# Hybrid decoder step on one core: order of splits, stores and bank copies in the first two feed-forward units

## The chip, the cores and the metric

The kernel runs on one core of a Trainium2 chip. The metric is the device time of one execution in microseconds (us); lower is better. The engines of the core run side by side, each with a queue of its own: TensorE (PE in the profile, its weight loads PEld), VectorE (DVE), ScalarE (ACT), GpSimd (POOL) and SyncE (SP). Nearly all transfers between the core's memory (SBUF) and the chip's main memory are issued from SP. PE writes its sums into eight banks of PSUM, which DVE and ACT read.

## The reference

One layer is computed for 2048 prompt rows and 64 sample rows of width 1024. After the attention half, each row x goes through a feed-forward half:

```
h = rms_norm(x, g_ffn_pre)
u = relu(h @ w_up)            # 1024 -> 4096
f = (u * u) @ w_down          # 4096 -> 1024
x = x + rms_norm(f, g_ffn_post)
```

All of it is float32. The change concerns the transition from the attention half to this one.

## The kernel before, in words

**Products in three parts.** A float32 matrix is split for PE into a high part (an ACT copy that rounds to the format of fast matmuls) and a low part (a DVE subtraction: original minus high part). A product is high*high + high*low + low*high, so each operand costs one ACT and one DVE instruction before PE can use it (split_by, L1610).

**Seven products for eight.** Both products of the feed-forward half use a seven-product scheme for 2x2 block matrices. The prompt rows are cut into two halves (sb = 0, 1) of 1024 rows; each half has 4 pairs of row tiles (row i and row i+4, 128 rows each). From the normed rows seven blocks H[1] to H[7] of 512 columns are made: four are the transposed rows themselves, three are differences; part p-1 of the row buffer ht holds block p. The weights w_up are taken 256 columns at a time (fc = 0 to 15). One (sb, fc) is a **unit**: seven products p = 1 to 7 of 12 matmuls each (up_product), p 0 and 8 being the sample rows' products and p 9 two transposes of these. Their banks appear in the profile as X (uX; products 1 and 2), Z (uc; 5 and 3), V (ud or ue by turns; 7 and 4) and Y (ua in unit 0, else ub; 6). Products 1 and 2 share a bank, as do 5 and 3, and 7 and 4; the sum after the first of them is read (by taken, L1751) before the second is added on top. So "copy X" is ACT's st<-uX, "copy Z" ACT's st<-uc. A unit's seven outputs lie in a buffer st (14 KB a partition): DVE adds up the sums (add), ACT takes relu and square (squared), and the buffer is stored to main memory (s_d) by end (L1838), which is run while the next unit's products go on.

**Weights of a unit.** Besides the two halves of the weights (which = 0 and 1; split_up, L1614) two pairs of sums are needed: sums_13, then, in the same tile, sums_24; each is split too (split_sums; tile names t and s in the profile). While unit fc runs, the function ahead (L1777) makes the weights of unit fc+1: "a" is the first half, "s13" and "s24" the sums, "13" and "24" their splits.

**Order of the queues.** te, ac and dv stand for PE, ACT and DVE with an order written out by hand: each instruction issued through them keeps its place behind the one issued before. Each engine works its queue strictly in order, so a waiting instruction holds up all that stand behind it. SP's transfers are put in order by the compiler, except where issue_after names one to follow. Waits between engines are put in by the compiler: for the data of a tile, and for a tile that takes the place of another in memory, for all users of the old one.

**The transition.** The rows come in the order 8, 12, 9, 13, 10, 14, 11, 15 for the second half, through residual (L1509): norm, 8 transposes on PE into two banks (xnT), two ACT copies from these to ht (L1536 to L1544), and for the second row of a pair four DVE differences (L1549 to L1551), then a store of ht to main memory (h_d, L1557). For each pair a new ht is taken, in the same place of pool keep as the one before (L1530), so that its first copies wait for the store. The last two rows overlap with unit 0 (sb 0, fc 0), whose order is UP_FIRST = 1, 0, 2, 8, 5, 7, 9, 6, 3, 4 and whose side work is written out in opening (L1847):
- row 11's two copies are put off (late_copies, L1542) and run at product 2, behind the first up weights' split
- row 15 (last_rows) is taken a step at a time: scaling at products 1 and 0, transposes and copies at 5, two differences at 7, the others and the store at 9
- blocks 7, 6, 3 and 4 of the first half's rows, stored earlier, are fetched and split in that order. Block 4 is fetched (L1882) into the place where its own low part will lie, H[4][1], and split in place (L1589). H[4]'s two tiles lie one behind the other in pool h_4, which takes, with h_3, the place of the row pools x (16 KB) and s (statistics of the rows) once these are closed (L1873 to L1875), and room behind them
- at product 4 the weight sums "s24", their split, and the split of the second up weights of unit 1 follow.

Unit 1 is the one case where st lies in keep, where ht was (L1741). Units 1 to 15 use UP_ORDER = 1, 5, 7, 0, 6, 8, 3, 2, 9, 4; unit 1's product 1 is issued by unit 0, behind its product 6.

Of the kernel before, what the change touches and what calls it, by code (L numbers as in the profile page):

```python
# [13 lines left out]
F32R = mybir.dt.float32r  # L14
# [127 lines left out]
def hybrid_step_kernel(ctx: ExitStack, tc: tile.TileContext, I, O):  # L142
# [1320 lines left out]

    def h_place(sb, p):

        H[p] = [h_pools[p].tile([P, KT // 2, BT], F32R, tag=f"h{p}{u}", name=f"H{p}{u}_{sb}", bufs=1) for u in range(2)]

    def open_pools(to, names, label, side="left"):
        to.update({name: open_pool(f"{label}_{name}", side) for name in names})
# [14 lines left out]
    def ht_place(name):  # L1484
        return keep.tile([P, 7, KT // 2, P], F32, tag="st", name=name, bufs=1)
# [23 lines left out]
    def residual(i, banks, tensor=nc.tensor, scalar=nc.scalar, vector=nc.vector):  # L1509

        n = rows(i)
        x = res_x.pop(i, None) or load_x(i)[0]
        ssq = sp.tile([P, 48], F32, tag="ssq", name=f"bssq_{i}", bufs=2)
        junk = sp.tile([P, D], mybir.dt.bfloat16, tag="junk", name=f"bjunk_{i}", bufs=1)
        x1 = R["x"].tile([P, D], F32, tag="x1", name=f"x1_{i}", bufs=2)
        if i == NB:
            banks = [folded(x1[:NS, c * 512 : (c + 1) * 512], p_) for c, p_ in enumerate(banks)]
        if banks:
            g = g_mix if tensor is nc.tensor else [gpost[:, c * 512 : (c + 1) * 512] for c in range(2)]
            yield from mixed(i, banks, x, x1, junk, ssq, g, sp, scalar, vector)  # L1520
        rs = ssq[:, 3:5]
        scalar.activation(junk[:n], x[:n], AF.Square, accum_out=ssq[:n, 2:3])
        yield
        rsqrt_mean(sp, rs[:n, 1:2], ssq[:n, 2:3], n, D, vector=vector)
        vector.scalar_tensor_tensor(x1[:n], x[:n], rs[:n, 1:2], gpre[:n], op0=ALU.mult, op1=ALU.mult)
        yield
        sb, j, second = i // 8, i % 4, i % 8 >= 4
        q = slice(j * P, (j + 1) * P)
        if i < NB and not second and i:
            sums[sb, j] = ht_place(f"ht_{i}")  # L1530
        for h in range(2):
            kk = slice(h * 4, h * 4 + 4)
            pt = (bank([P, 512], "ce"[h], f"xnT_{i}_{h}") if te is tensor else next_bank("cdce", f"xnT_{i}_{h}")).rearrange("p (k t) -> p k t", k=4)
            for k in range(4):
                tensor.transpose(pt[:, k, :n], x1[:n, (h * 4 + k) * P : (h * 4 + k + 1) * P], ident[:n, :n])
            if i == NB:  # L1536
                split_copy(xsT[:, kk, :NS], xsT[:, kk, NS:], pt[:, :, :NS], vector)
                continue
            ht = sums[sb, j]
            copy = (ht[:, (6, 2)[h] if second else h], pt, AF.Copy)  # L1540
            if i == B_ORDER[-2]:
                late_copies.append(copy)  # L1542
            else:
                scalar.activation(*copy)  # L1544
            if sb == 0 and not second:
                split_copy(H[h + 1][0][:, :, q], H[h + 1][1][:, :, q], pt, vector)
        if i == NB or not second:
            return
        yield  # L1549
        for out, a, b in ((4, 6, 0), (6, 2, 6), (5, 2, 4), (3, 1, 5)):  # L1550
            vector.tensor_tensor(ht[:, out], ht[:, a], ht[:, b], op=ALU.subtract)  # L1551
            if out == 6 and i == B_ORDER[-1]:
                yield
        kept = slice(2 * (sb == 0), 7)
        if i == B_ORDER[-3]:
            yield
        latest_store[:] = [nc.sync.dma_start(h_d[sb][:, kept, :, q], ht[:, kept])]  # L1557

    h_raws = {}

# [49 lines left out]
    def split_by(scalar, vector, hi, lo, src):  # L1610
        scalar.activation(hi, src, AF.Copy)
        vector.tensor_tensor(lo, src, f32(hi), op=ALU.subtract)

    def split_up(sb, fc, which, scalar=nc.scalar, vector=nc.vector):  # L1614

        w = P if sb and not which else FC
        halves_[sb, fc, which] = parts = [
            U["ab"[which] + "hl"[u]].tile([P, KT // 2, w], F32R, tag="w", name=f"w{which}{u}_{sb}_{fc}", bufs=1) for u in range(2)  # L1620
        ]
        split_by(scalar, vector, *parts, raws[sb, fc][which][:, :, :w])

    for n, i in enumerate(B_ORDER[2:]):
        early.append((i, []))
# [101 lines left out]
    def up(sb, fc, before, steps=iter(())):  # L1727
# [20 lines left out]
        def add(out, a, b, op=ALU.add):  # L1748
            dv.tensor_tensor(s(out), a, b, op=op)
# [27 lines left out]
        def ahead(kind):  # L1777

            if last:
                return  # L1780
            if kind == "a":
                split_up(sb, fc + 1, 0, ac, dv)
            elif kind in ("13", "24"):
                split_sums(sb, fc + 1, int(kind), ac, dv)
            else:
                (sums_13 if kind == "s13" else sums_24)(sb, fc + 1, dv)
# [6 lines left out]
        for p in UP_FIRST if first else UP_ORDER:  # L1793
            if (sb, fc, p) == (0, 1, 1):
                pass
            elif 0 < p < 8:
                product(p)
            elif sb:
                continue
            elif p < 9:  # L1800
                sample_up(fc, p // 8, sam)
            if p == 3:
                add(6, s(1), Z)
            if first:
                opening(p, taken, ahead)
                if p == 3:
                    squared(s(6))
                elif p == 6:
                    next(features)
                continue  # L1810
            if p == 1:
                next(before, None)
                if fc > 1 or sb:
                    split_up(sb, fc, 1, ac, dv)
                if fc + 2 < NFC:
                    load_up(sb, fc + 2)
                deque(before, 0)
            if p == 3:
                ahead("24")
                squared(s(6))  # L1820
            else:
                taken(p)
            if p == 1:
                ahead("s13")
            elif p == 7:
                ahead("13")
            elif p == (6 if sb else 0):
                ahead("a")
            if p == 6:
                ahead("s24")  # L1830
            downs(p)
            run(steps, 2)
# [3 lines left out]
        run(features)  # L1836

        def end():  # L1838
            add(1, s(1), V)
            yield  # L1840
            squared(s(1))
            add(2, s(1), s(5), ALU.subtract)
            nc.sync.dma_start(s_d[sb][fc], place[0])

        return end()

    def opening(p, taken, ahead):  # L1847

        if p == 1:
            taken(p)  # L1850
            next(last_rows)
            loaded = placing[0]
            for n, raw in enumerate(h_raws[3]):
                with tc.issue_after(loaded.ins):
                    loaded = nc.sync.dma_start(raw, h_d[0][:, 2, 2 * n : 2 * n + 2])
            next(seventh)
        elif p == 0:
            next(last_rows)
            sums_24(0, 0, dv)
        elif p == 2:  # L1860
            taken(p)
            ahead("a")
            for copy in late_copies:
                ac.activation(*copy)
        elif p == 8:
            taken(p)
            split_sums(0, 0, 24, ac, dv)
            run(load_h(0, 6, ac, dv))
            U.pop("tmp").release()
        elif p == 5:  # L1870
            taken(p)
            next(last_rows)
            close_pools(R)  # L1873
            for q in H_LATE[3:]:
                h_pools[q] = open_pool(f"h_{q}")  # L1875
            ahead("s13")
            run(load_h(0, 3, ac, dv))
            h_place(0, 4)
            loaded = None
            for k in range(0, KT // 2, 2):  # L1880
                with tc.issue_after(loaded.ins) if loaded else nullcontext():
                    loaded = nc.sync.dma_start(f32(H[4][1][:, k : k + 2]), h_d[0][:, 3, k : k + 2])  # L1882
            with tc.issue_after(loaded.ins):
                latest_store[:] = [load_up(0, 2)]
        elif p == 7:
            taken(p)
            next(last_rows)
            split_in_place(4)
        elif p == 9:
            taken(p)  # L1890
            ahead("13")
            run(last_rows)
        elif p == 6:
            next_X.append(bank([P, BT], "a", "uX_0_1"))
            up_product(0, 1, 1, next_X[0])
            taken(p)
        elif p == 3:
            with tc.issue_after(latest_store[0].ins):
                for half in range(2):
                    load_down(0, half)  # L1900
        else:
            ahead("s24")
            ahead("24")
            split_up(0, 1, 1, ac, dv)

    def sample_up(fc, c, sam):

# [350 lines left out]
```

## Time and profile before

| what | us |
|---|---|
| median of 3 runs | 2193.89 |
| lowest and highest run | 2193.14, 2196.88 |
| the profiled execution | 2193.01 |
| its span, first to last instruction | 2191.2 |
| the first units in it, from unit 0's first product to unit 2's first | 879.52 to 930.60 |

A row of the profile names the source line, engine, operation and the tiles written and read (numbers left out: H stands for all blocks, st for all unit buffers). Many instructions have line L131, that of the helper which keeps the order by hand; they are told apart by their tiles. Times are microseconds from the first instruction. In a timeline the columns are start, length, engine, line, operation and tiles, and the count that a row merges; brackets give the idle time of the engine just before, and what ended it. In a table of windows they are the stretch, its length, the busy time of PE, PEld, DVE, ACT and POOL (with counts), the granted clock of PE, the busy share of the transfer engines and the rate in GB/s. In a list of waits they are who waited for whom, the sum in us, how often, and the longest.

### The profile page before, as it was taken

What the parts mean: (1) busy time and instruction counts of PE and PEld (TensorE: products, weight loads), DVE (VectorE), ACT (ScalarE), POOL (GpSimd) and SP (SyncE); (2) the same over time, 40 slices, a digit from 0 to 9 for tenths busy, and PEclk for the clock granted to TensorE, in tenths of its full rate; (3) what the DMA queues carried; (4) which work ended last, traced back from release to release, by engine and by line L of the source; (5) the groups of instructions that cost most, each with busy time, mean ns of one, the idle gap of its engine ahead of it and who ended that gap; (6) DMA issues with size and microseconds to landing.
All of it is one profiled execution on the core that took longest, in us unless ns stands there. A gap on an engine that the chain in (4) does not pass through costs nothing.

```text
span 2191.2 us, 34210 instructions
## 1 busy us (share of the span) xinstructions
PE 2156.9 (98%) x11784; PEld 1864.8 (85%) x11784; DVE 1530.7 (70%) x3199; ACT 1219.1 (56%) x2626; POOL 257.7 (12%) x414
## 2 busy tenths in 40 slices
PE   8999999999999999999999999999999999999998
PEld 7999989999998888788888887888888888888886
DVE  5988968777785765888888555548676666555566
ACT  5888867566664444555555544435445455444454
POOL 2566512121111100000000000000000000000000
PEclk9999999999999999999999999999999999999999
DMA  7344332224337765877777776758554433766685
GB/s 229 133 144 150 103 104 66 68 71 150 131 126 239 235 205 193 263 240 257 272 258 249 249 237 220 242 181 269 179 182 158 153 136 134 241 202 195 194 271 185
DMA packets 240314, 411.54 MB, mean 188 GB/s; under 512 B 25924, under 2 KB 142124, under 8 KB 236028
## 3 DMA queue, kind: packets, MB, share of 16 engines
q1 hardware_dynamic: 240140, 409.35, 56.6%
q8 instruction: 93, 1.52, 0.3%
q14 instruction: 81, 0.66, 0.1%
HBM read 265.82 MB, written 143.99 MB: 187 GB/s over the span
## 4 chain that ended last, share of the span: by engine, by line
PE 89%; ACT 3%; DVE 3%; DMA 2%; POOL 1%; issue 1%; SPq 0%; DVEq 0%; POOLq 0%; ACTq 0%
PE dn L131 27%; PE gproj L131 11%; PE uc L131 8%; PE uX L131 7%; PE out L1328 7%; PE proj L131 5%; PE ud L131 4%; PE ub L131 4%; PE ue L131 4%; PE sam L131 1%; PE dsam L131 1%; PE o L131 1%; PE sc L131 1%; PE out L131 1%; PE av L131 1%; PE pT L131 1%
## 5 line engine op out<-in xcount | busy, mean ns | idle before, releaser
L131 PE MATMUL dn<-o0t,o0s 128*128 128x512 f32 x896 | 349.3, 390 | 2.1 <-ACT f L2026 1.0
L131 PE MATMUL dn<-o1t,o0s 128*128 128x512 f32 x896 | 349.6, 390 | 0.7 <-DVE o1t L220 0.7
L131 PE MATMUL dn<-o0t,o1s 128*128 128x512 f32 x896 | 349.4, 390 | 0.0
L220 DVE TENSOR_TENSOR o1s<-rs,o0s 128x512 fp32r<-128x512 f32 x224 | 154.6, 691 | 230.9 <-ACT o0s L219 225.1
L219 ACT ACTIVATE o0s<-rs 128x512 fp32r<-128x512 f32 x224 | 141.1, 631 | 305.3 <-PE dn L131 285.4
L131 PE MATMUL gproj<-wg,gxh 128*128 128x384 f32 x1024 | 272.5, 342 | 0.3 <-DVE gp_s L214 0.3
L131 PEld LDWEIGHTS dn<-o0t,o0s 128*128 128x128 f32 x896 | 168.2, 188 | 39.8 <-ACT o0t L219 1.6
L131 ACT ACTIVATE st<-st 128x512 f32<-128x512 f32 x224 | 141.2, 630 | 106.7 <-DVE st L131 101.9
L131 PEld LDWEIGHTS dn<-o1t,o0s 128*128 128x128 f32 x896 | 168.2, 188 | 37.7 <-DVE o1t L220 1.9
L131 PEld LDWEIGHTS dn<-o0t,o1s 128*128 128x128 f32 x896 | 168.2, 188 | 35.3
L131 PE MATMUL uc<-H,s 128*128 128x512 f32 x768 | 187.8, 393 | 2.8 <-ACT st L131 2.8
L131 PEld LDWEIGHTS gproj<-wg,gxh 128*128 128x128 f32 x1024 | 183.8, 188 | 4.1 <-issue 3.1
L131 PE MATMUL gproj<-wg,gxl 128*128 128x384 f32 x576 | 186.0, 340 | 0.4 <-DVE gp_s L214 0.4
L131 PE MATMUL uX<-H,w 128*128 128x512 f32 x768 | 185.5, 390 | 0.0
L131 PEld LDWEIGHTS uc<-H,s 128*128 128x128 f32 x768 | 143.7, 189 | 33.6 <-ACT st L131 3.0
L131 PEld LDWEIGHTS uX<-H,w 128*128 128x128 f32 x768 | 144.4, 188 | 30.5
L220 DVE TENSOR_TENSOR o1t<-rt,o0t 128x512 fp32r<-128x512 f32 x224 | 153.1, 684 | 9.0 <-ACT o0t L219 9.0
L1328 PE MATMUL out<-wo,mt 128*128 128x512 f32 x680 | 158.6, 392 | 0.0
L209 POOL TENSOR_TENSOR frs<-rs_v,half 128x1 f32<-128x1 f32 (+1 forms) x13 | 10.1, 786 | 1208.7 <-DMA rt<-t_d 1119.0
L1328 PEld LDWEIGHTS out<-wo,mt 128*128 128x128 f32 x680 | 126.5, 188 | 26.1
L219 ACT ACTIVATE o0t<-rt 128x512 fp32r<-128x512 f32 x224 | 138.1, 618 | 12.0 <-DMA rt<-t_d 8.5
L131 DVE TENSOR_TENSOR st<-st 128x512 f32<-128x512 f32 x160 | 110.6, 691 | 28.5 <-ACT st L131 24.3
(405 smaller groups left out, 4306.9 us busy)
## 6 DMA issues: line engine op xcount, KB each, us to landing
s_d<-st SPq DMA_DIRECT2D x32, 1792.0 KB, 8.1
rs<-s_d SPq DMA_DIRECT2D x224, 256.0 KB, 2.9
raw<-in_w_up SPq DMA_DIRECT2D x64, 512.0 KB, 4.4
rt<-t_d SPq DMA_DIRECT2D x128, 256.0 KB, 3.9
rt<-in_w_down SPq DMA_DIRECT2D x96, 256.0 KB, 3.0
t<-in_w_down SPq DMA_DIRECT2D x64, 256.0 KB, 3.8
t_d<-t SPq DMA_DIRECT2D x32, 512.0 KB, 4.2
hraw<-h_d SPq DMA_DIRECT2D x20, 512.0 KB, 5.1
```

The lines of the kernel that those rows point to most:

```text
L131: ins = call(*a, **k)
L209: nc.gpsimd.tensor_tensor(out, v[:n], e, op=ALU.pow)
L219: nc.scalar.activation(hi, src, AF.Copy)
L220: vector.tensor_tensor(lo, src, f32(hi), op=ALU.subtract)
L1328: te.matmul(banks[c], x, w[:, c * 512 : (c + 1) * 512], start=k + u == 0, stop=k == KT - 1 and u == len(products) - 1,)
```

## The change

- In the second row half, the pairs share one ht (no new one per pair). Parts 0 and 1 are stored as soon as the first row of a pair is copied, parts 2 to 6 after the second row; row 11's parts 0 and 1 are stored in opening. The first half's store is as it was (parts 2 to 6).
- Row 11's late copies go from product 2 to product 1, ahead of copy X.
- H[4]'s two tiles are placed in the other order, so that the fetch fills the one that lies first.
- Row 15's first two differences go from product 7 to 5 (ahead of the sums s13 and block 3's split), the last two still stand at product 9, now behind "s24", which comes up from product 4.
- The sums with Y and Z (taken(6), s(6)) and their squares go from products 6 and 3 to product 4, behind the split of the "24" weights. Of the second up weights' split, the ACT part stands ahead of them and the DVE part (split_low) behind; then comes the sum with V, which was in end.
- In unit 1, end's squares, difference and store of unit 0 go from product 1 (ahead of copy X) to product 5 (behind copy Z).

```diff
 h_place(sb, p):
-        H[p] = [h_pools[p].tile([P, KT // 2, BT], F32R, tag=f"h{p}{u}", name=f"H{p}{u}_{sb}", bufs=1) for u in range(2)]
+        H[p] = [
+            h_pools[p].tile([P, KT // 2, BT], F32R, tag=f"h{p}{u}", name=f"H{p}{u}_{sb}", bufs=1)
+            for u in ((1, 0) if (sb, p) == (0, 4) else (0, 1))
+        ]
+        if (sb, p) == (0, 4):
+            H[p].reverse()
 residual:
-            sums[sb, j] = ht_place(f"ht_{i}")
+            sums[sb, j] = sums[sb, j - 1] if sb and j else ht_place(f"ht_{i}")
         if i == NB or not second:
+            if i < NB and sb and i != B_ORDER[-2]:
+                nc.sync.dma_start(h_d[sb][:, :2, :, q], ht[:, :2])
             return
-        kept = slice(2 * (sb == 0), 7)
-        latest_store[:] = [nc.sync.dma_start(h_d[sb][:, kept, :, q], ht[:, kept])]
+        latest_store[:] = [nc.sync.dma_start(h_d[sb][:, 2:, :, q], ht[:, 2:])]
 split_up:
-        split_by(scalar, vector, *parts, raws[sb, fc][which][:, :, :w])
+        src = raws[sb, fc][which][:, :, :w]
+        if vector is None:
+            scalar.activation(parts[0], src, AF.Copy)
+        else:
+            split_by(scalar, vector, *parts, src)
+
+    def split_low(sb, fc, which, vector):
+        hi, lo = halves_[sb, fc, which]
+        vector.tensor_tensor(lo, raws[sb, fc][which], f32(hi), op=ALU.subtract)
 up:
-            if p == 3:
+            if p == 3 and not first:
                 add(6, s(1), Z)
             if first:
-                opening(p, taken, ahead)
-                if p == 3:
+                opening(p, taken, ahead, lambda out, a, b: add(out, s(a), {"Z": Z, "V": V}[b]))
+                if p == 4:
                     squared(s(6))
...
-                deque(before, 0)
+                if fc > 1 or sb:
+                    deque(before, 0)
...
+            elif p == 5:
+                deque(before, 0)
 end:
-            add(1, s(1), V)
+            if not first:
+                add(1, s(1), V)
 opening:
         if p == 1:
+            for copy in late_copies:
+                ac.activation(*copy)
+            nc.sync.dma_start(h_d[1][:, :2, :, 3 * P :], sums[1, 3][:, :2])
             taken(p)
...
         elif p == 2:
             taken(p)
             ahead("a")
-            for copy in late_copies:
-                ac.activation(*copy)
...
         elif p == 5:
             taken(p)
+            next(last_rows)
             next(last_rows)
...
         elif p == 7:
             taken(p)
-            next(last_rows)
             split_in_place(4)
         elif p == 9:
             taken(p)
             ahead("13")
+            ahead("s24")
             run(last_rows)
         elif p == 6:
             next_X.append(bank([P, BT], "a", "uX_0_1"))
             up_product(0, 1, 1, next_X[0])
-            taken(p)
...
         else:
-            ahead("s24")
             ahead("24")
-            split_up(0, 1, 1, ac, dv)
+            split_up(0, 1, 1, ac, None)
+            taken(6)
+            add(6, 1, "Z")
+            split_low(0, 1, 1, dv)
+            add(1, 1, "V")
```

More of the change, by code (lines that the diff above doesn't have):

```diff
@@ L1845, in up, with opening @@
         return end()
-    def opening(p, taken, ahead):
+    def opening(p, taken, ahead, add):
         if p == 1:
+            for copy in late_copies:
+                ac.activation(*copy)
+            nc.sync.dma_start(h_d[1][:, :2, :, 3 * P :], sums[1, 3][:, :2])
             taken(p)
```

## The prediction

> **What bounds the kernel now.** I read the page's share of busy time first, then the chain that ended last.
>
> ```profile
> span 2191.2 us, 34210 instructions
> PE 2156.9 (98%) x11784; PEld 1864.8 (85%) x11784; DVE 1530.7 (70%) x3199; ACT 1219.1 (56%) x2626; POOL 257.7 (12%) x414
> ...
> PE 89%; ACT 3%; DVE 3%; DMA 2%; POOL 1%; issue 1%; SPq 0%; DVEq 0%; POOLq 0%; ACTq 0%
> ```
>
> TensorE (PE) is busy 98% of the span, so an edit to the other engines counts only where PE stands still. The change touches the first two units (blocks 0 and 1 of the first row half, about 879 to 931 us). There I read PE's timeline; the bracket is the idle time before a group and what ended it.
>
> ```profile
> 890.93 1.14 PE L131 MATMUL xnT<-ident,x 128*128 128x128 f32 x8 [1.00 <-ACT ht L131]
> ...
> 897.64 2.92 PE L131 MATMUL uX<-H,w 128*128 128x512 f32 x12
> ...
> 912.88 0.73 PE L131 MATMUL ub<-H,s 128*128 128x512 f32 x2 [0.45 <-ACT s L131]
> 914.14 2.57 PE L131 MATMUL ub<-H,s 128*128 128x512 f32 x10 [0.53 <-DVE s L131]
> ...
> 920.42 4.34 PE L131 MATMUL uc<-H,s 128*128 128x512 f32 x12 [2.77 <-ACT st L131]
> 924.56 3.23 PE L131 MATMUL uX<-H,w 128*128 128x512 f32 x12
> ...
> 930.60 2.88 PE L131 MATMUL uX<-H,w 128*128 128x512 f32 x12
> 933.32 2.90 PE L131 MATMUL uc<-H,s 128*128 128x512 f32 x12
> ...
> 951.89 2.88 PE L131 MATMUL uX<-H,w 128*128 128x512 f32 x12
> ```
>
> Four stops: 1.00 + 0.45 + 0.53 + 2.77 = 4.75 us. They cost more than that. From 930.60 to 951.89 one whole unit without a stop takes 21.29 us, and a product of twelve matmuls 933.32 - 930.60 = 2.72. From 897.64 to 930.60 PE does one unit and two products more (p3 and p4 of unit 0): 21.29 + 2 x 2.72 = 26.7, but it takes 32.96. So 6.2 us are lost there, and 1.0 at 890.93: **7.2 us** in all, 0.33% of the time. That is the ceiling of what the change can gain, because PE waits for nothing else in reach of it. The windows show what makes 7.2 out of 4.75.
>
> ```profile
> 918.10:920.42 2.32, 0.00 (x0) 0.00 (x0) 0.99 (x2) 2.23 (x4) 0.00 (x0) 1.00 1.08 351
> 920.42:924.76 4.34, 4.33 (x13) 3.45 (x14) 3.75 (x5) 2.27 (x3) 0.00 (x0) 0.66 1.03 420
> ```
>
> After the last stop the granted clock (third number from the right) is 0.66: the product at 920.42 takes 924.56 - 920.42 = 4.14 instead of 2.72, 1.4 us more, and the next some 0.3; the other 0.7 is the refilling of the pipeline at the stops. [...]
>
> **The change, part by part.** Queues of the engines are worked through in program order, by the spacings that the rows show: a VectorE (DVE) subtraction of 128x1024 takes 1.15 us of its queue, a pair of 128x512 about 1.3; on ScalarE (ACT) 1.0 and 0.5. ACT now:
>
> ```profile
> 882.57 0.60 ACT L131 ACTIVATE st<-uX 128x512 f32<-128x512 f32 x1 [1.06 <-PE uX L131]
> ...
> 890.28 1.09 ACT L131 ACTIVATE ht<-xnT 128x512 f32<-128x512 f32 x2 [1.80 <-DMA h_d<-ht]
> ...
> 891.51 1.07 ACT L131 ACTIVATE s<-t 128x1024 fp32r<-128x1024 f32 x1
> ...
> 899.98 1.06 ACT L131 ACTIVATE H<-H 128x1024 fp32r<-128x1024 f32 x1 [2.14 <-DMA H<-h_d]
> 901.83 1.06 ACT L131 ACTIVATE H<-H 128x1024 fp32r<-128x1024 f32 x1 [0.79 <-DMA H<-h_d]
> ...
> 918.11 1.29 ACT L131 ACTIVATE st<-st 128x512 f32<-128x512 f32 x2 [3.45 <-DVE st L131]
> 919.31 0.58 ACT L131 ACTIVATE st<-uX 128x512 f32<-128x512 f32 x1
> 919.78 0.59 ACT L131 ACTIVATE st<-uc 128x512 f32<-128x512 f32 x1
> ```
>
> *Row store in two parts, bank copies first.* The two copies at 890.28 (row 11) need a new row buffer, hence the landing of row 14's whole store, which is in the chain of waits:
>
> ```profile
> 881.10 9.16 DMA h_d<-ht
> ...
> 896.51 5.30 DMA H<-h_d
> ```
>
> PE's transposes of row 15 need the banks that those copies empty: that is the stop of 1.00. After the change the copies write parts 0 and 1 of the same buffer, stored long before for row 10; they wait only for row 14's subtractions (over at 881.1) and stand ahead of the uX copy, in the 1.06 us in which ACT waits for PE anyway: about 881.5 to 882.6. Without that cover they would cost 1.0. Gain **1.0**. The added stores (one each for rows 8 to 11, a quarter of a us to half a us of SP issue) carry bytes that the whole store no longer carries; the ones for rows 8 to 10 lie beside out products in which PE never stops, so I take 0. The store for row 11 stands in front of row 15's x store on SP, with no more bytes ahead of block 3's fetch than now.
>
> *Fourth block into the other half.* SP now:
>
> ```profile
> SPq L1882 <- DVE H L131: 6.3, 1, 6.3
> ```
> ```profile
> 860.69 0.55 SPq L1557 DMA_DIRECT2D h_d<-ht  x1
> ...
> 887.85 1.95 SPq L1855 DMA_DIRECT2D st<-h_d  x2
> 896.14 0.79 SPq L1882 DMA_DIRECT2D H<-h_d  x2
> ...
> 906.68 0.53 SPq L1557 DMA_DIRECT2D h_d<-ht  x1
> ```
>
> The fetch waits 6.3 us for the split of block 6, since the tile that it fills lies on that block's staging pool. By the code H[4]'s first tile begins where the pool of row statistics began, last used by row 15's scaling before 889; with the order turned, the fetch lands there. It can go right behind block 3's, about 890 (6 us earlier), and both ACT waits (2.14, 0.79) end. Transfers from SP follow each other: the engines fell idle as block 3 was in,
>
> ```profile
> 861.00:862.00 1.00, 1.00 (x6) 0.83 (x5) 0.75 (x1) 0.16 (x1) 0.00 (x0) 1.00 0.07 19
> 867.00:868.00 1.00, 1.00 (x6) 0.81 (x5) 0.23 (x2) 0.00 (x0) 0.54 (x1) 1.00 0.97 290
> ...
> 894.00:895.00 1.00, 1.00 (x7) 0.80 (x5) 1.00 (x2) 1.00 (x3) 0.00 (x0) 1.00 0.05 20
> ```
>
> so block 4 follows from 894 and is in at 897.5 (1 MB at some 350 GB/s), as ACT comes to it. By itself the edit buys no PE time; it clears the queue for the next step. If block 3's and 4's bytes mixed instead, see the third case.
>
> *Order of splits, sums and squares.* DVE now:
>
> ```profile
> 888.94 0.68 DVE L131 TENSOR_TENSOR t<-t,raw 128x512 f32<-128x512 f32 x1
> ...
> 892.62 1.23 DVE L131 TENSOR_TENSOR s<-t,s 128x1024 fp32r<-128x1024 f32 x1 [1.14 <-ACT s L131]
> 893.76 2.35 DVE L131 TENSOR_TENSOR H<-hraw,H 128x1024 fp32r<-128x1024 f32 x2
> ...
> 900.10 1.41 DVE L131 TENSOR_TENSOR ht<-ht 128x512 f32<-128x512 f32 x2
> ...
> 905.21 1.41 DVE L131 TENSOR_TENSOR ht<-ht 128x512 f32<-128x512 f32 x2
> ...
> 912.87 1.23 DVE L131 TENSOR_TENSOR s<-t,s 128x1024 fp32r<-128x1024 f32 x1 [1.19 <-ACT s L131]
> 914.01 1.22 DVE L131 TENSOR_TENSOR w<-raw,w 128x1024 fp32r<-128x1024 f32 x1
> ...
> 917.40 0.68 DVE L131 TENSOR_TENSOR st<-st,ud 128x512 f32<-128x512 f32 x1
> ```
>
> No DVE instruction is added, and on ACT none. Without the late copies in front, ACT makes the high part at 891.51 about 1.2 earlier (it needs the sums, over at 890.3), so the low part at 892.62 runs at 891.4 and block 6's at 892.6 to 894.9. PE is by then 1.0 earlier: the cover stays. Then DVE does, in the new order, row 15's first two differences (1.3), next weight sums (1.3), block 3 (2.3), V (0.6), block 4 (2.3), the 13 weights (1.15), the 24 sums (1.3) and the last differences (1.3): 11.6 us, till **906.4**. Row 15's store goes there, 0.3 before the 906.68 of now. The 24 weights' low part (ACT's high part is ready at 906) ends at 907.8; PE wants it at 912.88 - 0.45 - 1.0 = 911.4 (where it now begins to wait, less the first gain). Slack 3.6: the stops of 0.45 and 0.53 go. Then three sums of unit 0 (2.0) and the low part of the second up weights (1.15): 910.9, against PE's want at 911.4 + 2.72 = 914.1.
>
> What is late next is the stop at 920.42. PE waits there for the copy of Z (uc, 919.78), queued on ACT behind two squares (918.11), which wait 3.45 us for the V sum (917.40). In the new order ACT has the X copy and the Z copy before those squares. But the X copy opens unit 1's buffer, which lies where the row buffer lay: **a wait is added**, the landing of row 15's store, and behind it on ACT the Z copy, then the squares; PE waits for Z. The trace does not show that wait. It is bounded by two stores: 9.16 us for the one at 881.10, amid other transfers, and for the one at 860.69, alone: 1.25 us until the first byte (0.07 of slice 861 to 862), then 1.835 MB at 290 GB/s, 6.3, and some 0.5 until the waiter ran. The new store has 5 of 7 parts and finds the engines idle: 1.25 + 4.5 + 0.5 = 6.3. I take this, the nearer row: 906.4 + 6.3 = 912.7, Z copied at 913.8, and PE comes for it at 915.1 (914.1 and the samples: now from 916.7, the end of the group at 914.14, to 920.42 - 2.77 = 917.65). Slack 1.3 us. With 9.16 it is 916.7, a stop of 1.6.
>
> After that unit 1's X, Z and V sums have no new wait, and unit 0's store to memory leaves near 916 rather than 920; its buffer is next written in unit 2.
>
> **Sum:** 1.0 + 6.2 = 7.2 us. The profiled execution: span 2191.2, time 2193.01, so 2185.8; the median of the runs shown, 2193.89, is 0.88 above, and from it the forecast is **2186.7 us**.
>
> **The rivals.**
> 1. *The row buffer is late.* Store landing in 9.16, or leaving 1 to 3 us later: PE stops 1.6 to 3 us for Z, and from about 2.8 pays the slow clock (1.7) again. Gain 5.5 down to 2.5: 2188.4 to 2191.4, the shorter stops likelier, so about 2189.2. For it: slack of only 1.3. Against: the engines are empty at 906.
> 2. *DVE or ACT becomes the bound.* If block 4 and the next weights (2 MB, now issued near 890) share the engines with block 3 instead of following it, block 3 is in near 900 instead of 894; ACT and DVE stand in line behind its split, and PE's p3 of unit 0 stops 3 to 4 us, with the slow clock: 7.2 - 5.2 = 2.0, 2191.9. Against: the idle slice at 894.
> 3. *It doesn't do what it says:* the other half also touches the staging pool and the fetch goes near 895. Then block 4 is split some 1 us later, inside the slacks: still 2186.7 to 2187. It is no case of its own and counts with the forecast.
> 4. *Slower.* If the wait goes by the whole row buffer and not by its parts, the copies at the head of unit 0 hold ACT until row 14's store has landed, 890.25, and now the uX copy stands behind them: X is copied at 891.9, PE's second uX product waits from 883.3, 8.6 us, then the slow clock, 1.7. 10.3 lost against 7.2 won: +3.1, 2197.0 (a longer cold spell: up to 2199). It is slower as soon as that landing is after 887.3. Against: block 4's two halves were split each at its own transfer's end (2.14 and 0.79), so waits go by parts.
>
> **How the numbers follow.** Forecast 0.62, first rival 0.16, second 0.12, fourth 0.07, other things 0.03. The range goes from 2185.5 (all of it, and 1.2 from shorter tails) to 2191.7, in the second rival's middle: left out are the fourth, half the second and a little below, about 0.18. About 0.2% (4.4 us, below 2189.5) is what a measurement of this kernel can tell from no change. Faster: 0.62 + 0.11 of the first = 0.73. Within: 0.05 of the first, 0.12, half of the fourth = 0.20. Slower: the rest of the fourth and of the others, 0.07.
>
> **What would show it.** ACT's ht copies near 881.5 with no DMA wait, and no stop before PE's transposes; the H fetch on SP near 890; row 15's store near 906; the copy of uc near 913.5, ahead of the squares; clock 1.00 in every slice from 880 to 930; unit 2's first uX near 923.4. A PE stop at p3 of unit 1 speaks for the first rival, one at p3 of unit 0 for the second, one before the second uX for the fourth.

## The result, and the profile after

The changed kernel takes 2188.85 us (median of 9 runs, 2186.53 to 2191.24), the kernel before, run in turn with it, 2193.89 us (9 runs, 2191.23 to 2201.41). The ratio is **0.9973, 95% interval 0.9962 to 0.9985**: 3.3 to 8.3 us faster. The forecast of 2186.7 us, 7.2 below the median shown, lies inside the interval; the median came out 2.15 us above it.

The profiled execution of the changed kernel took 2191.24 us, the longest of its nine. First the page: the span, the share of the engines, and the chain that ended last.

```profile
span 2189.5 us, 34228 instructions
...
PE 2157.9 (99%) x11784; PEld 1866.5 (85%) x11784; DVE 1531.0 (70%) x3199; ACT 1218.4 (56%) x2626; POOL 257.8 (12%) x414
...
PE 89%; ACT 4%; DVE 4%; DMA 2%; issue 1%; POOL 1%; DVEq 0%; SPq 0%; POOLq 0%; ACTq 0%
```

PE's work is the same 11784 matmuls. The span is only 1.7 us shorter, so the page alone would say that most of the gain failed to come. The first two units say otherwise. This is PE's timeline of the changed kernel there:

```profile
881.52 3.02 PE L131 MATMUL uX<-H,w 128*128 128x512 f32 x12
...
891.78 1.03 PE L131 MATMUL xnT<-ident,x 128*128 128x128 f32 x8
...
898.49 2.92 PE L131 MATMUL uX<-H,w 128*128 128x512 f32 x12
...
913.12 2.91 PE L131 MATMUL ub<-H,s 128*128 128x512 f32 x12
...
917.17 3.03 PE L131 MATMUL uc<-H,s 128*128 128x512 f32 x12 [0.19 <-ACT st L131]
920.04 2.88 PE L131 MATMUL uX<-H,w 128*128 128x512 f32 x12
...
925.74 2.88 PE L131 MATMUL uX<-H,w 128*128 128x512 f32 x12
```

Of the four brackets of before (1.00, 0.45, 0.53, 2.77) one is left, of 0.19. I call the time from unit 0's first uX to unit 2's first uX **the stage**. It took 930.60 - 879.52 = 51.08 us before and takes 925.74 - 881.52 = 44.22 now, **6.86 less**; the prediction had unit 2 begin at 923.4, so 43.9. PE's clock (third number from the right in a table of windows) stays at 1.00 in it:

```profile
880.00:900.00 20.00, 20.00 (x105) 16.82 (x105) 18.39 (x25) 15.70 (x24) 1.08 (x2) 1.00 1.05 345
900.00:915.00 15.00, 15.00 (x72) 12.50 (x71) 14.61 (x19) 7.49 (x13) 0.00 (x0) 1.00 0.58 171
915.00:930.00 15.00, 14.81 (x70) 12.20 (x69) 12.17 (x18) 9.17 (x15) 0.00 (x0) 1.00 0.75 267
390.00:400.00 10.00, 10.00 (x75) 9.22 (x75) 6.32 (x18) 5.83 (x18) 1.64 (x2) 0.85 0.09 25
1520.00:1530.00 10.00, 7.94 (x28) 6.10 (x27) 8.37 (x14) 4.92 (x8) 0.00 (x0) 0.83 0.58 196
```

The last two rows are where this execution gave time back, both far from the change. At 390 to 400 PE is busy throughout, small matmuls among its work, but at a clock of 0.85; before, that stretch had 1.00. The stage starts 2.0 us later than before, so every time in it is to be read 2.0 later than in the prediction. The other loss is a stop in the second half's down products, where the same wait was 0.36 us before, with a clock of 0.83 around it:

```profile
1523.13 0.63 PE L131 MATMUL dn<-o0t,o0s 128*128 128x512 f32 x1 [2.06 <-DVE f L1976]
```

Together, 2.0 later before the stage, 6.86 won in it, and 3.2 lost behind it (the remainder) make the 1.7. Whether these losses belong to the change is the first question for the experiments.

ACT's timeline of the changed kernel answers to the one shown of before:

```profile
881.52 2.00 ACT L131 ACTIVATE H<-hraw 128x1024 fp32r<-128x1024 f32 x2
883.41 1.07 ACT L131 ACTIVATE ht<-xnT 128x512 f32<-128x512 f32 x2
884.58 0.60 ACT L131 ACTIVATE st<-uX 128x512 f32<-128x512 f32 x1
...
899.00 1.06 ACT L131 ACTIVATE H<-H 128x1024 fp32r<-128x1024 f32 x1 [0.29 <-DMA H<-h_d]
900.26 1.06 ACT L131 ACTIVATE H<-H 128x1024 fp32r<-128x1024 f32 x1 [0.20 <-DMA H<-h_d]
...
911.31 2.48 ACT L131 ACTIVATE st<-st 128x512 f32<-128x512 f32 x4 [1.91 <-DVE st L131]
...
916.03 0.60 ACT L131 ACTIVATE st<-uX 128x512 f32<-128x512 f32 x1 [1.36 <-DMA h_d<-ht]
916.53 0.59 ACT L131 ACTIVATE st<-uc 128x512 f32<-128x512 f32 x1
917.01 1.29 ACT L131 ACTIVATE st<-st 128x512 f32<-128x512 f32 x2
```

The two ht copies at 883.41 wait for nothing and fill the time in which ACT waited for PE. The copy of Z (uc) stands ahead of the squares at 917.01. In front of it is the wait that the change adds: the copy of X waits 1.36 us for the landing of the row buffer's store. SP's timeline shows that store (908.68) and the fetch of block 4 (892.09):

```profile
884.51 3.59 SPq L1870 DMA_DIRECT2D h_d<-ht  x1
...
892.09 1.24 SPq L1902 DMA_DIRECT2D H<-h_d  x2
...
906.63 0.37 SPq L1613 DMA_DIRECT2D raw<-in_w_up  x1
908.68 0.37 SPq L1563 DMA_DIRECT2D h_d<-ht  x1
```

The chain that ended last in this stretch runs through the store, once:

```profile
907.93 0.70 DVE ht L131
908.63 0.02 SPq L1563
908.65 0.03 issue
908.68 7.27 DMA h_d<-ht
...
916.03 1.09 ACT st L131 x2
917.13 0.04 issue
917.17 3.03 PE uc L131 x12
```

The store took 7.27 us, not the 6.3 forecast, and left 0.3 us later in the stage than forecast; so the slack of 1.3 us became a stop of 0.19. Two us ahead of it SP had issued another transfer, the first half of unit 3's up weights (0.5 MB, at 906.63). Before, both halves of these weights left behind the store, at 914.85; now the sums that free their place are made earlier.

### The profile page after: what moved, and what is told of

It reads as the page before. It is cut to its first block, busy times and chain, and to the rows that moved or that the text cites. A ratio compares the mean times of both kernels' runs of the same rounds, so it can differ in the third digit from the quotient of the medians.

```text
span 2189.5 us, 34228 instructions
## 1 busy us (share of the span) xinstructions
PE 2157.9 (99%) x11784; PEld 1866.5 (85%) x11784; DVE 1531.0 (70%) x3199; ACT 1218.4 (56%) x2626; POOL 257.8 (12%) x414
## 4 chain that ended last, share of the span: by engine, by line
PE 89%; ACT 4%; DVE 4%; DMA 2%; issue 1%; POOL 1%; DVEq 0%; SPq 0%; POOLq 0%; ACTq 0%
PE dn L131 27%; PE gproj L131 11%; PE uc L131 8%; PE uX L131 7%; PE out L1328 7%; PE proj L131 5%; PE ud L131 4%; PE ub L131 4%; PE ue L131 4%; PE sam L131 1%; PE dsam L131 1%; PE o L131 1%; PE sc L131 1%; PE out L131 1%; PE av L131 1%
```

## The experiments

In every expectation A is the account that the prediction gave; the other letters are the rivals, named there. The runs e1 to e4 were timed in turn with the kernel before at 2193.41 us (24 runs), e5 to e8 at 2194.14 (23 runs).

| run | median us (runs) | ratio, 95% | stage us | PE's stops in the stage |
|---|---|---|---|---|
| changed kernel | 2188.85 (9) | 0.9973 (0.9962 to 0.9985) | 44.22 | 0.19 |
| e1 changed, again | 2186.57 (7) | 0.9973 (0.9962 to 0.9983) | 44.16 | none |
| e2 row store, early copies alone | 2190.48 (10) | 0.9986 (0.9976 to 0.9995) | 48.16 | 0.25, 0.53, 2.77 |
| e3 changed, old fetch place | 2186.56 (5) | 0.9968 (0.9956 to 0.9980) | 44.24 | none |
| e4 order alone | 2189.82 (10) | 0.9984 (0.9975 to 0.9993) | 47.63 | 1.45, 1.93 |
| e5 before, stop filled | 2193.13 (10) | 0.9994 (0.9985 to 1.0003) | 49.50 | 0.91, 0.53, 0.53 |
| e6 changed, a new buffer | 2196.11 (10) | 1.0009 (1.0000 to 1.0018) | 53.02 | 7.68 |
| e7 changed, end first | 2188.80 (6) | 0.9974 (0.9963 to 0.9985) | 44.14 | none |
| e8 changed, store first | 2186.32 (5) | 0.9965 (0.9952 to 0.9977) | 43.80 | none |

### e1: are the losses elsewhere the change's?

No edit: the changed kernel once more, five rounds.

> The changed kernel once more, unaltered. Stage (unit 0's first product to unit 2's first) 51.08 us before, 44.22 in the changed kernel's profile, so 6.9 us won there, while that profile's whole span is only 1.7 us shorter. Theory A (the loss elsewhere is chance: a clock dip near 395 us and a late transfer near 1520 us that come and go from run to run): stage 44.2 again, and at least one of the two losses absent or of another size; median gain 5 to 7 us. Rival B (the change itself brings the later stop: given back): stage 44.2 again, and the stop of about 2 us with a low clock near 1520 us is there again.

PE's timeline, the two ends of the stage:

```profile
879.69 3.02 PE L131 MATMUL uX<-H,w 128*128 128x512 f32 x12
...
923.85 2.88 PE L131 MATMUL uX<-H,w 128*128 128x512 f32 x12
```

The stage is 44.16 us again, while the span falls to 2184.8: at the down products the stop is 0.5 instead of 2.06. A loss of that size behind the stage is thus not in every execution of the changed kernel. The sixteen runs of the changed kernel taken together have a median of 2187.2 (**the pooled median**). The rival, that the gain is given back later, is not borne out here; e7 shows such a stop once more. The lowered clock at 390 to 400 appears in ten of all fourteen profiles, of the old order and of the new (the kernel before among them, in e9 to e11); where it is absent the stage starts at 878.3 to 879.5 us, where it is present at 878.7 to 881.9.

### e2 and e4: the two halves of the change alone

e2 is the kernel before with the row store in parts and the early copies:

```diff
 residual:
-            sums[sb, j] = ht_place(f"ht_{i}")
+            sums[sb, j] = sums[sb, j - 1] if sb and j else ht_place(f"ht_{i}")
...
+            if i < NB and sb and i != B_ORDER[-2]:
+                nc.sync.dma_start(h_d[sb][:, :2, :, q], ht[:, :2])
...
-        kept = slice(2 * (sb == 0), 7)
...
-        latest_store[:] = [nc.sync.dma_start(h_d[sb][:, kept, :, q], ht[:, kept])]
+        latest_store[:] = [nc.sync.dma_start(h_d[sb][:, 2:, :, q], ht[:, 2:])]
 opening:
         if p == 1:
+            for copy in late_copies:
+                ac.activation(*copy)
+            nc.sync.dma_start(h_d[1][:, :2, :, 3 * P :], sums[1, 3][:, :2])
             taken(p)
...
             ahead("a")
-            for copy in late_copies:
-                ac.activation(*copy)
```

> Kernel before with the row store in two parts and row 11's copies first, nothing else. Theory A (only the stop at row 15's transposes hangs on the row store): stage 50.1, so 1.0 less than before; the stops at ub and at uc of unit 1 stay within 0.3 us, clock low after the last one. Rival C (the late copies were what held ACT and DVE up, so that everything behind them comes earlier): the later stops shrink too and the stage is below 48.5.

e4 is the changed kernel with just these lines, and the place of block 4, put back: the new order alone.

```diff
 h_place:
-            for u in ((1, 0) if (sb, p) == (0, 4) else (0, 1))
...
+        H[p] = [h_pools[p].tile([P, KT // 2, BT], F32R, tag=f"h{p}{u}", name=f"H{p}{u}_{sb}", bufs=1) for u in range(2)]
 residual:
-            sums[sb, j] = sums[sb, j - 1] if sb and j else ht_place(f"ht_{i}")
+            sums[sb, j] = ht_place(f"ht_{i}")
...
-            if i < NB and sb and i != B_ORDER[-2]:
-                nc.sync.dma_start(h_d[sb][:, :2, :, q], ht[:, :2])
...
-        latest_store[:] = [nc.sync.dma_start(h_d[sb][:, 2:, :, q], ht[:, 2:])]
+        kept = slice(2 * (sb == 0), 7)
+        latest_store[:] = [nc.sync.dma_start(h_d[sb][:, kept, :, q], ht[:, kept])]
 opening:
         if p == 1:
-            for copy in late_copies:
-                ac.activation(*copy)
-            nc.sync.dma_start(h_d[1][:, :2, :, 3 * P :], sums[1, 3][:, :2])
...
         elif p == 2:
             taken(p)
             ahead("a")
+            for copy in late_copies:
+                ac.activation(*copy)
```

> Changed kernel with the row store, the late copies and H[4]'s place as before: only the order of splits, sums and squares is changed. Theory A: the stop of 1.0 at row 15's transposes is back, the stops at ub stay away, and the X copy of unit 1 now waits for the landing of a whole row store (some 9 us after its issue, against 7.3): Z about 2 us late, a stop of 2 to 3 us at uc of unit 1, with a low clock if it is over 2.5; stage 47 to 49.5. Rival C (the order alone brings it): stage 45.2, with the 1.0 alone.

In e2 the stop ahead of the transposes is gone and the last one stands as it was, but the clock behind it does not:

```profile
918.88 3.04 PE L131 MATMUL uc<-H,s 128*128 128x512 f32 x12 [2.77 <-ACT st L131]
```

```profile
918.00:924.00 6.00, 5.12 (x22) 4.22 (x23) 5.38 (x8) 3.11 (x5) 0.00 (x0) 1.00 0.73 306
```

The same 2.77 us of idling, and the product behind it is done in 921.76 - 918.88 = 2.88 instead of 4.14. The stage of 48.16 is not A's 50.1, and it is below the rival's 48.5 without the rival's reason, since the last stop did not shrink. It is the stops (0.25 + 0.53 + 2.77 = 3.55), the 43.9 of a stage without stops, and a rest of 0.7 like the one that the prediction put down to refilling (its estimate; no run shows what makes the rest up). Of the 1.9 that A has too much, 1.7 is the clock and 0.2 the stop that shrank from 0.45 to 0.25. Neither theory had the clock; e9 to e12 take it up.

In e4 the first stop is back and the last is down to 1.93, held by the store, as ACT's timeline shows:

```profile
917.84 0.60 ACT L131 ACTIVATE st<-uX 128x512 f32<-128x512 f32 x1 [3.01 <-DMA h_d<-ht]
```

The store, issued at 908.84, is of all seven parts here and lands 9.0 us later, not 7.3, with the same 0.5 MB of weights issued 2.1 us ahead of it. The stage of 47.63 lies in A's 47 to 49.5, not at the rival's 45.2. At equal clock the halves can be compared with e10 below, a profile of the kernel before with 1.00 behind its last stop and a stage of 49.13: the rows alone win 1.0, the order alone 1.5, both together 4.9. Neither half does it alone; the order needs the shorter store, which comes from the other half. By the times e2 gains 2.9 us (1.1 to 5.3), more than its 1.0; nothing in e2 shortens its last stop, so where the rest comes from stays open.

### e3: the place of block 4

```diff
 h_place, from the changed kernel:
-        H[p] = [
-            h_pools[p].tile([P, KT // 2, BT], F32R, tag=f"h{p}{u}", name=f"H{p}{u}_{sb}", bufs=1)
-            for u in ((1, 0) if (sb, p) == (0, 4) else (0, 1))
-        ]
-        if (sb, p) == (0, 4):
-            H[p].reverse()
+        H[p] = [h_pools[p].tile([P, KT // 2, BT], F32R, tag=f"h{p}{u}", name=f"H{p}{u}_{sb}", bufs=1) for u in range(2)]
```

> Changed kernel with H[4] placed in the old order, so that block 4's fetch waits for block 6's split again. Theory A (the new place buys no PE time by itself): fetch issued about 5 us later, ACT's two splits of block 4 wait 1 to 2 us, stage 44.2 to 44.9. Rival D (the early fetch is what lets DVE be in time): a PE stop of 1 us or more comes back and the stage is above 45.5.

ACT's timeline has the old waits back:

```profile
897.57 1.06 ACT L131 ACTIVATE H<-H 128x1024 fp32r<-128x1024 f32 x1 [2.11 <-DMA H<-h_d]
899.21 1.06 ACT L131 ACTIVATE H<-H 128x1024 fp32r<-128x1024 f32 x1 [0.58 <-DMA H<-h_d]
```

PE does not stop, the stage is 44.24 and the median that of e1. The earlier fetch takes most of two waits from ACT and buys no PE time, as A has it (of the waits that A put at 1 to 2 us the second is shorter).

### e5: the last stop filled with work

The kernel before, with product 6 of unit 1 computed twice (24 matmuls, 12 of them to fill the stop):

```diff
             elif 0 < p < 8:
+                if (sb, fc, p) == (0, 1, 6):
+                    product(p)
                 product(p)
```

> Kernel before, in which product 6 of unit 1 is computed twice into the same bank (12 matmuls more, same result), so that PE works through the time of its 2.77 us stop and comes to uc when the Z copy is just done. Theory A (the idle stop is what lowers the clock): no stop at uc, granted clock 1.00 behind it, stage 51.08 - 1.7 = 49.4 in spite of 12 more matmuls. [...]

PE's timeline:

```profile
914.77 5.30 PE L131 MATMUL ub<-H,s 128*128 128x512 f32 x22 [0.53 <-DVE s L131]
919.91 1.11 PE L131 MATMUL sam<-w,xsT 128*128 128x256 f32 x8
921.05 3.03 PE L131 MATMUL uc<-H,s 128*128 128x512 f32 x12
```

Twelve matmuls more and the stage is not longer but shorter, 49.50 where A says 49.4; the clock stays at 1.00. Since e2 shows that the clock can stay up behind the stop too, this one profile supports A without deciding, and the ratio's interval holds 1.

### e6: the fourth rival made true

The changed kernel, but row 11's pair takes a new row buffer in the old place, so that its early copies wait for row 14's store:

```diff
-            sums[sb, j] = sums[sb, j - 1] if sb and j else ht_place(f"ht_{i}")
+            sums[sb, j] = sums[sb, j - 1] if sb and j in (1, 2) else ht_place(f"ht_{i}")
```

> Changed kernel in which row 11 gets a row buffer of its own in the old place, so that its copies, still at the head of ACT's queue, wait for row 14's store to land: the fourth rival of the prediction made true. Theory A (its price): copies about 7 to 9 us behind unit 0's first product instead of 1.9, the second uX product stops 5.5 to 8.5 us, then a low clock worth 1.7; stage 51.5 to 54.5, so 0.5 to 3.5 us slower than before. Rival F (slack further back takes up part of it): stage below 50.5.

ACT's and PE's timelines:

```profile
889.69 1.09 ACT L131 ACTIVATE ht<-xnT 128x512 f32<-128x512 f32 x2 [8.02 <-DMA h_d<-ht]
```

```profile
891.32 4.39 PE L131 MATMUL uX<-H,w 128*128 128x512 f32 x12 [7.68 <-ACT st L131]
```

This is the rival as it was priced: the copies hold ACT 8.02 us and PE's second product stops 7.68 where the prediction said 8.6. The stage is 53.02, 8.8 longer than with the shared buffer (prediction 10.3), and the whole 1.97 us slower than before (interval 0 to 3.9; prediction 3.1). Early copies without the shared buffer bring nothing, and by the median they lose 2 us.

### e7: unit 0's end back at its old place

```diff
-                if fc > 1 or sb:
-                    deque(before, 0)
+                deque(before, 0)
...
-            elif p == 5:
-                deque(before, 0)
```

> Changed kernel in which unit 0's last squares, difference and store stand ahead of unit 1's X copy again. Theory A (X waits for the row store's landing anyway, and the V sum is now done before it, so the squares fit into that wait): stage 44.2 to 44.5. Rival G (the order of squares and bank copies is what removes the stop at uc): Z copied 1 us later or more, a stop of 1 us or more at uc, stage above 45.2.

No stop, stage 44.14, a median (2188.8, 6 runs) equal to the changed kernel's. It is not the place of unit 0's end that counts, as A has it. Its profile shows the stop at the down products again, 2.91 us with a clock of 0.83 about it, as the first profile of the changed kernel had.

### e8: unit 3's weights behind the store

```diff
-                    load_up(sb, fc + 2)
+                    with tc.issue_after(latest_store[0].ins) if (sb, fc) == (0, 1) else nullcontext():
+                        load_up(sb, fc + 2)
```

> Changed kernel in which the fetch of unit 3's weights is ordered behind row 15's store. In the changed kernel half of that fetch (0.5 MB) goes out 2 us ahead of the store, and the store lands 7.3 us after its issue where 6.3 was worked out. Theory A (the half fetch ahead of it is the difference): landing 6.2 to 6.5 us after the issue, the X copy 0.9 earlier, no stop at uc (0.19 now), stage 44.0; time within 0.1% of the changed kernel. Rival H (this store takes that long by itself): landing 7.0 or more.

SP's and ACT's timelines:

```profile
906.04 0.37 SPq L1563 DMA_DIRECT2D h_d<-ht  x1
```

```profile
912.78 0.60 ACT L131 ACTIVATE st<-uX 128x512 f32<-128x512 f32 x1 [0.75 <-DMA h_d<-ht]
```

With nothing issued just ahead of it the store lands 6.7 us after its issue, in this one profile, against 7.3 in three (changed kernel, e1, e3): between A's 6.2 to 6.5 and the rival's 7.0 or more, nearer to A. The weights ahead of it explain 0.6 of the 1.0 us that the prediction missed. This is the fastest kernel of the study by its median, and its stage (43.80) the shortest, but its interval overlaps that of the changed kernel: not shown to be better.

### e9 to e12: does the slow clock belong to the stop?

No edit: four more single executions of the kernel before.

> The kernel before, unaltered, looked at again. Its first profile showed a stop of 2.77 us at uc of unit 1 and a granted clock of 0.66 behind it; the kernel with the row store in two parts alone showed the same stop of 2.77 us and a clock of 1.00. Theory A (the stop itself lowers the clock each time): stop 2.8, clock low, stage 51.1 in each look. Theory W (whether the clock falls depends on when the stop lies, which differs from run to run): stops as before, but in some of the four looks the clock stays at 1.00 and the stage is 49.3 to 49.5.

> Second look at the kernel before. Theory A: stage 51.1 and a low clock behind the stop at uc. Theory W: either 51.1 with a low clock or 49.4 without.

> Third look at the kernel before. Theory A: stage 51.1 and a low clock behind the stop at uc. Theory W: either 51.1 with a low clock or 49.4 without.

> Fourth look at the kernel before. Theory A: stage 51.1 and a low clock behind the stop at uc. Theory W: either 51.1 with a low clock or 49.4 without.

Their times are 2195.45, 2192.49, 2190.92 and 2192.94 us, their stages 51.18, 49.13, 50.84 and 51.09; single times differ by more than the clock is worth, so only the stages are compared. PE's timeline of e10 and then of e11, each followed by a window about the product behind the stop:

```profile
915.12 2.57 PE L131 MATMUL ub<-H,s 128*128 128x512 f32 x10 [0.53 <-DVE s L131]
...
921.40 3.03 PE L131 MATMUL uc<-H,s 128*128 128x512 f32 x12 [2.77 <-ACT st L131]
```

```profile
921.00:925.00 4.00, 3.60 (x16) 2.98 (x17) 3.41 (x6) 2.62 (x4) 0.00 (x0) 1.00 1.08 429
```

```profile
913.03 2.56 PE L131 MATMUL ub<-H,s 128*128 128x512 f32 x10 [0.53 <-DVE s L131]
...
919.31 4.61 PE L131 MATMUL uc<-H,s 128*128 128x512 f32 x12 [2.77 <-ACT st L131]
```

```profile
919.20:923.76 4.56, 4.45 (x12) 3.53 (x13) 3.97 (x6) 2.33 (x4) 0.00 (x0) 0.63 1.06 429
```

From ub on the two have the same stops to the hundredth (0.17 before the first group of ub in both, 0.53, 2.77), and the clock behind them is 1.00 in one and 0.63 in the other; e9 (0.62 from 922.86 to 927.30) and e12 (0.66 from 919 to 924) go with e11. So in four of five profiles of the kernel before the stop cost some 1.7 us more than its own length, in one of five, and in e2, it did not. That is the rival's answer, not A's.

Read in windows of 0.1 us, the clock stood at 0.50 from 921.8 to 925.2 us in the first profile of before, and from 397.0 to 400.4 and from 1523.4 to 1526.8 in that of the changed kernel: 3.4 us at half the clock each time, which costs 1.7. In windows of 10 us e9 and e11 lose the same 1.7 (0.83 from 920 to 930), so does e12 (0.96 and 0.87 from 910 to 930), and with the 7.68-us stop of e6 it is twice that (0.87 and 0.79 from 880 to 900).

Why the clock fell behind the 2.77-us stop in four executions and not in e10 and e2 was not shown. The rival's reason, when the stop lies, fits both outcomes, but it is the author's estimate: no run moved a stop on purpose.

## Why the prediction was right, point by point

- **What bounds.** Right: with the four stops gone PE has no wait left in the stage but the 0.19 (none in e1), and the stage fell to its ceiling within 0.3 us (44.22 against 43.9).
- **Row store and early copies, 1.0 us.** Right. The copies start 1.9 us after the stage's start (forecast 2.0), the stop of 1.00 is gone in e2 and back, as 1.45, in e4. That waits go by parts of the buffer shows in the copies themselves: they start 0.3 us after the issue of row 14's store (883.10), wait for no transfer, and write parts of the same buffer that this store leaves out. With a buffer of its own (e6) the same copies wait 8.02 us.
- **Block 4's place, 0 us.** Right: the fetch goes 10.6 us after the stage's start (forecast 10.5), and e3 without it is as fast. The third rival was, as said, no case of its own; the second did not come: ACT's waits for blocks were 0.29 and 0.20.
- **Order on DVE.** Right for the splits: the 24 weights' low part, 1.22 us from 908.74, is done 3.2 us ahead of PE's first use at 913.12, where the slack was put at 3.6. Row 15's store left 27.16 us into the stage in both kernels; the 0.3 us earlier did not come.
- **The added wait, 6.3 us.** Mis-sized by 1.0: 7.27 (7.28 in e1). "Finds the engines idle" was the wrong step: SP's queue was not worked out for the new order, in which a fetch for unit 3 has moved ahead of the store. Without it 6.7 (e8). The forecast slack of 1.3 went to the landing (1.0) and to the store's 0.3; with PE 0.1 us earlier than forecast, the stop of 0.19 is what is left. The first rival was thus partly true, and cost 0.19 us. That it cost no more is luck in part: the two errors happened to be as large as the slack.
- **The clock, 1.7 us.** The mis-sized term of the sum. The 3.4 us at a clock of 0.50 behind the stop cost the 1.7, but the prediction read one execution and counted its slow clock as part of every run of before. Behind the same stop e10 and e2 ran at 1.00. The stage of before is some 51.05 us in four profiles and 49.13 in one, against 44.2 now: 6.85 or 4.9 to win, 6.5 on average if four in five is the true share, which makes 2193.89 - 6.5 = 2187.4, beside the pooled median of 2187.2. The lengths from which the clock was to fall, "about 2.8" in the first rival and 2.5 in what was expected of e4, were the author's estimates, and no run shows such a length: behind a stop of 2.06 (changed kernel, at 1523) the clock fell to 0.50, behind those of 2.77 in e10 and e2 it stayed.
- **From the stage to the time.** The forecast fits the pooled median within 0.5 us; the median of the first nine runs stood 2.15 above it. In the profiles losses of about 2 us come and go elsewhere: the clock at 390 to 400, and the stop at the down products, 0 to 2.9 us in the seven profiles with the new order of splits, 0 to 1.8 in the seven with the old. That these made the 2.15 is likely but not shown, since only profiled executions show them. Why that stop is long in one run and short in the next stays open, and so does whether the change makes it longer.

## What to carry to other kernels

Measure a stop by what the stage takes without it (two stretches of equal work, one with and one without), not by its bracket, and read the clock behind it in more than one execution before counting that as won: the same stop of 2.77 us cost 1.7 us more or nothing more. When a change adds a wait on a transfer, list what the queue issues in the two microseconds ahead of it: here 0.5 MB ahead made up about 0.6 of the 7.3 us. A copy brought forward is only free if its target's last reader is done; the same edit with another buffer (e6) cost 8.8 us.

## What the runs showed of the hardware

- The granted clock stood at 0.50 for 3.4 us behind the 2.77-us stop of the first profile of before (921.8 to 925.2), and for 3.4 us twice in the changed kernel's profile (397.0 to 400.4, 1523.4 to 1526.8).
- The same 2.77-us stop of PE (2.78 in e9), behind short stops of 0.17 to 0.45 and of 0.53 (0.52 in e9), was followed by a low clock in four executions (0.62 to 0.66 in windows of 4.3 to 5.0 us: before, e9, e11, e12) and by 1.00 in two (e2, e10). Stops of 2.06 (changed kernel) and 2.91 (e7) at the down products went with a clock of 0.83 from 1520 to 1530, stops of 1.3 (e5) and 1.78 (e12) there with 1.00, as did the 1.93 of e4 in the stage.
- The clock fell without any stop of PE in a stretch of small matmuls, at 390 to 400 us (0.83 to 0.89 in windows of 10 us), in ten of fourteen profiles.
- A store of 1.31 MB landed 6.7 us after its issue with nothing just ahead of it (e8) and 7.3 with 0.5 MB issued 2 us earlier (changed kernel, e1, e3); one of 1.835 MB, also with 0.5 MB ahead, took 9.0 (e4).
